# Four or three of eight pairs of row tiles by seven block products, two of the weight sums by accumulating transfers, the second norm's rows on GpSimd's queue, and the hand-over to the MLP in another order

## The chip, the cores and the metric

The kernel runs on one core of a Trainium2 chip. A core has five engines, each with its own in-order queue of instructions: TensorE (PE, matrix products; its weight loads are listed apart as PEld), VectorE (DVE), ScalarE (ACT), GpSimd (POOL) and SyncE (SP, which here only issues transfers). Sixteen DMA engines move data between the device memory and the on-chip memory SBUF; products are summed in a second on-chip memory, PSUM. The metric is the device time of one execution in microseconds. The kernel before takes 1110.16 us, the median of three runs between 1109.35 and 1111.19.

## The reference

One encoder layer over 256 tokens of width 2048 in float32. The part that the change touches is the end of the cross attention, the norm behind it and the MLP:

```
xa = memory_cross_attention(x, layer_norm(mem))          # 4 heads, 256 memory tokens
x  = layer_norm(ALPHA * x + xa)                          # the second norm, "ln2"
ff = jnp.square(jax.nn.relu(x @ w_mlp_in)) @ w_mlp_out   # 2048 -> 8192 -> 2048
x  = layer_norm(ALPHA * x + ff)
```

## The kernel before

**Three products for one.** A float32 matrix product is made of three products of operands split in a rounded high part and a rest: high by high, high by low, low by high. `split` (L78) makes the parts of a tile: ScalarE copies the high part (L80), VectorE subtracts it from the source for the low part (L81). `mm3` (L145) issues the three matmuls. So every weight passes through ScalarE and VectorE once before TensorE uses it. The split weights lie in four buffers each of `w_hi` and `w_lo`, 1024 columns wide.

**The MLP.** The 8192 hidden columns go in four chunks of 2048. For each chunk, four hidden groups (`hidden_group`, L854) compute 512 hidden columns each, transposed, as `ht`: per step of 128 rows of the input, four matmuls of 512 columns and four of 256 (`cols_wide`, L195 and L200). Then two pair products (`pair_product`, L904) multiply the chunk's `ht` into one half (1024 columns) of the output each; in the last chunk the second half goes another way (`w_ml`). A pair product runs over the chunk's sixteen row tiles in eight pairs, called units here. Within a unit, tokens (two blocks of 128), row tiles (two) and columns (two blocks of 512) form a 2 x 2 by 2 x 2 block product. Plainly that is eight block products of three matmuls each. For the units that `SEVEN` (L810) lists, Strassen's scheme in Winograd's form takes seven block products, with sums of blocks of `ht` (`sums_h`, made once per chunk in `hidden`, L832) and sums of blocks of the weights (made by VectorE in `load_unit`, L886). Before, units 2, 5 and 7 of both halves go by seven.

**The weight sums.** A unit's weights are one transfer of 128 x 2048 float32 (1 MB): the blocks b12, b11, b22, b21, 512 columns each. A seven unit needs b11 + b12 and b22 + b12 (one instruction over 1024 columns), that first sum plus b22 (512), and that plus b21 (512). They go into one of two buffers of 2048 columns in `wx`, and then through `split` like weights. The seven unit splits 1024 + 512 + 1024 + 1024 columns, a plain one twice 1024. Transfers of unit p + 2 are issued when unit p begins; the adds are queued then and taken one at a time behind each split (`part`, L893).

**The hand-over.** Between cross attention and the first hidden group stands the second norm. Its work is written out by hand and kept in this order (`pin`): the last cross products (L698) with their sums and statistics per token block (`add_cross`); mean and reciprocal root per block, the root on GpSimd (`moments_pinned`, L702 to L709); `scale2(b, n)` (L716), which normalises columns 512 n to 512 n + 511 of token block b in place on VectorE; `turn2(b, p)` (L728), two transposes on TensorE of the columns of pair p; `convert(p)`, gain and bias of the two transposed tiles (`gain2`, L733 on ScalarE, L735 on VectorE) and their split into `x2t` (L745, or L80 and L81). Pair p covers columns 256 p to 256 p + 255, so that pairs 4 and 5 need the scaled columns n = 2. `first_pair(p)` runs behind the matmuls of input tiles 2 p and 2 p + 1 of the first hidden group: it transposes pairs 2 and 3 of block 1 (p = 0), then pairs 4 to 7. Ten matmuls on a tile of ones (L768) fill TensorE's wait for the moments of block 1.

**The rest of the order.** What isn't pinned is placed by a scheduler that goes by estimated times. `residual("ln2")` (L544) applies gain and bias of the second norm to `res` in 512 columns at a time, with both rows loaded into scratch tiles by SyncE (L551); its pieces are taken one by one behind the splits of the first chunk.

## Time and profile before

| what | value |
|---|---|
| median of three runs | 1110.16 us |
| the profiled execution, its own time | 1108.42 us |
| its span, first to last instruction | 1106.6 us |
| TensorE busy, matmuls | 1091.8 us, 99%, 5951 |
| VectorE busy | 861.1 us, 78% |
| ScalarE busy | 587.3 us, 53% |
| GpSimd busy | 35.6 us, 3% |
| DMA, mean | 195 GB/s, queue share 54.5% of 16 engines |

The profile is one execution. Times within it are microseconds from its first instruction. Matmuls follow each other in a pipeline, so that the busy time of one (389 ns for 512 columns in the groups) is longer than the distance between two; the distance is read from the chain of waits. The chain is the work that ended last, followed back from the last instruction through whatever released it.

### The profile page before, as it was taken

To read this page: it belongs to the slowest core of one execution; us is meant where nothing else is said; L and a number is where in the kernel's file an instruction comes from. 1 tells how busy PE (TensorE), PEld (TensorE's weight loads), DVE (VectorE), ACT (ScalarE), POOL (GpSimd) and SP (SyncE) were. 2 spreads that over 40 slices of the span, in tenths; PEclk is the share of its full clock that TensorE was granted. 3 is DMA by queue.
4 is the path that set the end of the run, shared out by engine and by line. 5 is a ranking of instruction groups with operands and counts; after the bars stand their busy time and mean duration, and the time that the engine had idled before them with its cause. 6 is when DMAs were issued, how large, how long until landed. Compare 5 with 4: busy or idle time off the path is not lost.

```text
span 1106.6 us, 15304 instructions
## 1 busy us (share of the span) xinstructions
PE 1091.8 (99%) x5951; PEld 944.8 (85%) x5951; DVE 861.1 (78%) x1261; ACT 587.3 (53%) x860; POOL 35.6 (3%) x45
## 2 busy tenths in 40 slices
PE   9999999999999999999999999999999999999996
PEld 6988899988999878888888888888888888888885
DVE  6878677688879678888977678978668887678796
ACT  6455566545576435455655445555445555545550
POOL 1402000000100000000000000000000000000000
PEclk9999999999999999999999999999999999999998
DMA  9664453467567318744556555455554556555372
GB/s 333 234 227 142 156 193 127 174 220 247 180 205 272 145 44 299 266 166 181 192 223 221 184 185 209 181 200 192 198 183 175 204 200 223 186 191 190 115 255 87
DMA packets 37944, 215.86 MB, mean 195 GB/s; under 512 B 4336, under 2 KB 5232, under 8 KB 14192
## 3 DMA queue, kind: packets, MB, share of 16 engines
q1 hardware_dynamic: 37872, 214.89, 54.5%
q8 instruction: 46, 0.75, 0.3%
q14 instruction: 26, 0.21, 0.1%
HBM read 212.78 MB, written 2.10 MB: 194 GB/s over the span
## 4 chain that ended last, share of the span: by engine, by line
PE 98%; DVE 1%; DMA 0%; ACT 0%; issue 0%; POOL 0%; DVEq 0%; SPq 0%
PE acc L146 15%; PE acc L147 15%; PE acc L148 15%; PE acc L195 11%; PE att L195 11%; PE att L200 5%; PE acc L200 5%; PE att L147 3%; PE att L148 3%; PE att L146 3%; PE acc L188 2%; PE acc L186 2%; PE acc L187 2%; PE att L350 1%; PE acc L698 1%; PE att L528 1%
## 5 line engine op out<-in xcount | busy, mean ns | idle before, releaser
L81 DVE TENSOR_TENSOR w_lo<-raw,w_hi 128x1024 fp32r<-128x1024 f32 (+2 forms) x318 | 365.9, 1163 | 123.7 <-ACT w_hi L80 118.8
L80 ACT ACTIVATE w_hi<-raw 128x1024 fp32r<-128x1024 f32 (+2 forms) x318 | 317.9, 1011 | 266.0 <-PE acc L148 101.9
L80 ACT ACTIVATE w_hi<-wx 128x1024 fp32r<-128x1024 f32 x98 | 100.8, 1031 | 119.4 <-PE acc L148 85.5
L81 DVE TENSOR_TENSOR w_lo<-wx,w_hi 128x1024 fp32r<-128x1024 f32 x98 | 114.8, 1182 | 53.9 <-ACT w_hi L80 53.8
L195 PE MATMUL att<-x2t,w_hi 128*128 128x512 f32 x512 | 139.6, 394 | 0.0
L147 PE MATMUL acc<-w_lo,ht 128*128 128x512 f32 x354 | 137.8, 389 | 0.0
L148 PE MATMUL acc<-w_hi,ht 128*128 128x512 f32 x354 | 137.7, 389 | 0.0
L195 PE MATMUL acc<-x2t,w_hi 128*128 128x512 f32 x480 | 132.4, 394 | 0.0
L146 PE MATMUL acc<-w_hi,ht 128*128 128x512 f32 x354 | 111.5, 389 | 0.0
L195 PEld LDWEIGHTS att<-x2t,w_hi 128*128 128x128 f32 x512 | 88.0, 189 | 12.3
L195 PEld LDWEIGHTS acc<-x2t,w_hi 128*128 128x128 f32 x480 | 82.5, 189 | 11.5
L200 PEld LDWEIGHTS att<-x2t,w_lo 128*128 128x128 f32 x512 | 77.6, 189 | 10.3
L200 PEld LDWEIGHTS acc<-x2t,w_lo 128*128 128x128 f32 x480 | 73.3, 189 | 9.5
L200 PE MATMUL att<-x2t,w_lo 128*128 128x256 f32 x512 | 80.3, 281 | 0.0
L147 PEld LDWEIGHTS acc<-w_lo,ht 128*128 128x128 f32 x354 | 66.4, 188 | 14.0 <-DVE w_lo L81 0.2
L148 PEld LDWEIGHTS acc<-w_hi,ht 128*128 128x128 f32 x354 | 66.5, 188 | 13.8
L146 PEld LDWEIGHTS acc<-w_hi,ht 128*128 128x128 f32 x354 | 66.4, 188 | 13.8
L200 PE MATMUL acc<-x2t,w_lo 128*128 128x256 f32 x480 | 77.0, 281 | 0.0
L148 PE MATMUL acc<-w_hi,xt 128*128 128x512 f32 (+2 forms) x192 | 69.9, 365 | 0.0
L147 PE MATMUL acc<-w_lo,xt 128*128 128x512 f32 (+2 forms) x192 | 69.7, 364 | 0.0
L146 PE MATMUL acc<-w_hi,xt 128*128 128x512 f32 (+2 forms) x192 | 66.4, 366 | 0.8 <-ACT w_hi L80 0.8
L148 PE MATMUL acc<-w_hi,ot 128*128 128x512 f32 (+1 forms) x136 | 51.9, 382 | 0.0
(259 smaller groups left out, 1873.1 us busy)
## 6 DMA issues: line engine op xcount, KB each, us to landing
raw<-in_w_mi SPq DMA_DIRECT2D x64, 1024.0 KB, 4.9
wx<-in_w_mo SPq DMA_DIRECT2D x28, 1024.0 KB, 4.9
raw<-in_w_mo SPq DMA_DIRECT2D x28, 1024.0 KB, 4.8
raw<-in_w_out SPq DMA_DIRECT2D x16, 1024.0 KB, 4.9
raw<-in_w_ml SPq DMA_DIRECT2D x8, 1024.0 KB, 4.9
raw<-in_w_b SPq DMA_DIRECT2D x5, 1024.0 KB, 4.9
raw<-in_w_qa SPq DMA_DIRECT2D x16, 256.0 KB, 5.4
raw<-in_w_qa SPq DMA_DIRECT2D x4, 1024.0 KB, 4.8
```

The lines of the kernel that those rows point to most:

```text
L80: pin(nc.scalar.activation(hi, src, AF.Copy), pinned)
L81: return pin(nc.vector.tensor_tensor(out=lo, in0=src, in1=f(hi), op=ALU.subtract), pinned)
L146: nc.tensor.matmul(ps, ah, bh, start=start, stop=False)
L147: nc.tensor.matmul(ps, ah, bl, start=False, stop=False)
L148: nc.tensor.matmul(ps, al, bh, start=False, stop=stop)
L186: nc.tensor.matmul(ps, hi, xt[:, k, 0:S], start=k == 0, stop=False)
L187: nc.tensor.matmul(ps, hi, xt[:, k, S:2 * S], start=False, stop=False)
L188: nc.tensor.matmul(ps, lo, xt[:, k, 0:S], start=False, stop=k == nk - 1)
L195: pin(nc.tensor.matmul(ps, hi[:, i * P:(i + 1) * P], xt[:, k, :], start=k == 0, stop=k == nk - 1), pinned)
L200: pin(nc.tensor.matmul(ps[:, 0:S], lo[:, i * P:(i + 1) * P], xt[:, k, 0:S], start=False, stop=False), pinned)
L350: nc.tensor.transpose(pp[:, st * S + b * P:st * S + b * P + P], ev[:, b, st * P:(st + 1) * P], ident)
L528: nc.tensor.transpose(ps[:, o:o + P], x(b, k // 4)[:, (k % 4 + j) * P:(k % 4 + j + 1) * P], ident)
```

## The change

`SEVEN` becomes units 1, 3, 5, 7 of the first half and 3, 5, 7 of the second: 4 x 4 + 3 x 3 = 25 seven units where there were 7 x 3 = 21. `sums_h` holds four pairs.

The sums b11 + b12 and b22 + b12 are made by transfers: SyncE loads b12 twice, side by side, into one of three buffers of 1024 columns, and GpSimd issues a transfer with `accum_op=ALU.add` that adds b11 and b22 from the device memory onto it. `load_halves` does both; it is called before hidden groups 1, 2 and 3 of the first chunk and at the end of each seven unit, for the third seven unit ahead. A seven unit's own transfer leaves b12 out (768 KB). The other two sums stay on VectorE and go into one buffer, `t24`; they are queued during the unit before.

GpSimd's queue, and no longer SyncE's, issues the gain and bias rows of the second norm. In the hand-over `scale2(0, 2)` stands behind the moments of block 1, `scale2(0, 3)` in `first_pair(1)`, `scale2(1, 1)` ahead of `convert(0)` and `scale2(1, 2)` behind `convert(3)`; `convert(0)` uses another division of work between VectorE and ScalarE, `convert(1)` the general one; nine matmuls on ones stand where ten stood.

```diff
@@ residual @@
-                nc.sync.dma_start(rows[w], t[f"{name}_{w}"][n * 512:(n + 1) * 512].partition_broadcast(P))
+                (nc.gpsimd if name == "ln2" else nc.sync).dma_start(rows[w], t[f"{name}_{w}"][n * 512:(n + 1) * 512].partition_broadcast(P))
@@ moments_pinned(st, beside=None) @@
+        if beside is not None:
+            beside()
@@ convert @@
-        if p < 2:
-            for j in range(2):
-                k, o = 2 * p + j, slice(j * S, (j + 1) * S)
-                gain2(x2t[:, k, 0:S], ps[:, o], k, True)
-                gain2(y[:, o], ps[:, o], k, False)
-                pin(nc.vector.tensor_tensor(out=x2t[:, k, S:2 * S], in0=y[:, o],
-                                            in1=f(x2t[:, k, 0:S]), op=ALU.subtract), True)
+        if p == 0:
+
+            gain2(y[:, 0:S], ps[:, 0:S], 0, False)
+            gain2(y[:, S:2 * S], ps[:, S:2 * S], 1, True)
+            pin(nc.vector.tensor_copy(x2t[:, 0, 0:S], y[:, 0:S]), True)
+            pin(nc.scalar.activation(x2t[:, 1, 0:S], y[:, S:2 * S], AF.Copy), True)
+            for j in range(2):
+                pin(nc.vector.tensor_tensor(out=x2t[:, j, S:2 * S], in0=y[:, j * S:(j + 1) * S],
+                                            in1=f(x2t[:, j, 0:S]), op=ALU.subtract), True)
@@ the hand-over @@
-    scale2(0, 2)
-    scale2(0, 3)
     last = cross_mm(1, 3, 256, 256)
...
-    mom[1] = moments_pinned(sts[1])
+    mom[1] = moments_pinned(sts[1], lambda: scale2(0, 2))
...
     turn2(1, 1)
+    scale2(1, 1)
     convert(0)
-    scale2(1, 1)
     convert(1)
@@ first_pair @@
             convert(2)
+            convert(3)
             scale2(1, 2)
-            convert(3)
...
             if p == 1:
+                scale2(0, 3)
                 scale2(1, 3)
@@ the MLP @@
-    SEVEN = ((2, 5, 7), (2, 5, 7))
+    SEVEN = ((1, 3, 5, 7), (3, 5, 7))
...
+    sevens = deque(u for u in units if u[2] in SEVEN[u[1]])
+    t24 = sums_w[0][:, 0:1024]
+    spare = deque([sums_w[0][:, 1024:2048], sums_w[1][:, 0:1024], sums_w[1][:, 1024:2048]])
+
+    def load_halves():
+
+        if not sevens:
+            return
+        c, q, p = sevens.popleft()
+        s, src = spare[0], t["w_mo"][(c * 2 + q) * (CH // 2) + p]
+        spare.rotate(-1)
+        nc.sync.dma_start(s.rearrange("p (i c) -> p i c", i=2),
+                          src[:, 0:512][:, None, :].broadcast_to([P, 2, 512]))
+        nc.gpsimd.dma_start(s, src[:, 512:1536], accum_op=ALU.add)
+        halves.append(s)
@@ load_unit @@
+        o = 512 if seven else 0
+        nc.sync.dma_start(raw[:, o:], t["w_mo"][(c * 2 + q) * (CH // 2) + p][:, o:])
+        s, todo = None, []
         if seven:
-            add(s[:, 0:1024].rearrange("p (i c) -> p i c", i=2), raw[:, 512:1536].rearrange("p (i c) -> p i c", i=2),
-                b12[:, None, :].broadcast_to([P, 2, 512]))
-            add(s[:, 1024:1536], s[:, 0:512], b22)
-            add(s[:, 1536:2048], s[:, 1024:1536], b21)
+            s = halves.popleft(), t24
+            b22, b21 = raw[:, 1024:1536], raw[:, 1536:2048]
+            for o, a, b in ((t24[:, 0:512], s[0][:, 0:512], b22), (t24[:, 512:1024], t24[:, 0:512], b21)):
+                todo.append(lambda o=o, a=a, b=b: nc.vector.tensor_tensor(out=o, in0=a, in1=b, op=ALU.add))
```

What the scheduler makes of it, at three places. The first is VectorE at the start of the hand-over, from the statistics of columns 1536 to 1791 of token block 1 on; `res_1487` is token block 0, `res_1488` block 1. Before:

```order
L500 BN_STATS bn<-res_1488 128x6
L716 TENSOR_SCALAR res_1487<-res_1487,mv,rs_r 128x512 x2
L682 SCALAR_TENSOR_TENSOR res_1488<-res_1488,acc 128x256
L500 BN_STATS bn<-res_1488 128x6
L704 BN_AGGR mv<-bn 128x2
L706 TENSOR_SCALAR rs_v<-mv 128x1
L716 TENSOR_SCALAR res_1488<-res_1488,mv,rs_r 128x512
L735 TENSOR_SCALAR tmp<-att,gbt 128x256
L745 TENSOR_TENSOR x2t<-tmp,x2t 128x256
```

In the changed kernel, from the same statistics on:

```order
L500 BN_STATS bn<-res_1488 128x6
L682 SCALAR_TENSOR_TENSOR res_1488<-res_1488,acc 128x256
L500 BN_STATS bn<-res_1488 128x6
L704 BN_AGGR mv<-bn 128x2
L706 TENSOR_SCALAR rs_v<-mv 128x1
L718 TENSOR_SCALAR res_1487<-res_1487,mv,rs_r 128x512
L718 TENSOR_SCALAR res_1488<-res_1488,mv,rs_r 128x512 x2
L737 TENSOR_SCALAR tmp<-att,gbt 128x256
L746 CAST x2t<-tmp 128x256
L749 TENSOR_TENSOR x2t<-tmp,x2t 128x256 x2
```

The two scalings of block 0 that stood ahead of the last sum (L682) are gone from there: one stands behind the moments, the other much later. Two scalings of block 1 now stand together ahead of the first gain.

The second place is VectorE a little later, around the scaling of columns 1024 to 1535 of block 1 that pair 4 needs; each gain (`tmp<-att,gbt`) with the subtraction behind it is one `convert`. Before, from `convert(2)` on:

```order
L735 TENSOR_SCALAR tmp<-att,gbt 128x256
L81 TENSOR_TENSOR x2t<-tmp,x2t 128x2x256
L716 TENSOR_SCALAR res_1488<-res_1488,mv,rs_r 128x512
L735 TENSOR_SCALAR tmp<-att,gbt 128x256
L81 TENSOR_TENSOR x2t<-tmp,x2t 128x2x256
L81 TENSOR_TENSOR w_lo<-raw,w_hi 128x1024
```

In the changed kernel, from `convert(2)` on:

```order
L737 TENSOR_SCALAR tmp<-att,gbt 128x256
L81 TENSOR_TENSOR x2t<-tmp,x2t 128x2x256
L737 TENSOR_SCALAR tmp<-att,gbt 128x256
L81 TENSOR_TENSOR x2t<-tmp,x2t 128x2x256
L718 TENSOR_SCALAR res_1488<-res_1488,mv,rs_r 128x512
L81 TENSOR_TENSOR w_lo<-raw,w_hi 128x1024
```

The scaling moved from between `convert(2)` and `convert(3)` to behind both. On TensorE nothing moved there: the transposes of pair 4 stand behind the matmuls of input tiles 2 and 3 in both kernels.

The third place is the transfers of the first chunk. SyncE before, from the last of seven `w_mi` loads on:

```order
L134 DMA raw<-in_w_mi 128x2048 x7
L551 DMA tmp<-in_ln_g 128x512
L551 DMA tmp<-in_ln_b 128x512
L551 DMA tmp<-in_ln_g 128x512
L878 DMA wx<-in_w_mo 128x2048 x2
L134 DMA raw<-in_w_mi 128x2048
```

SyncE in the changed kernel, from the same loads on:

```order
L134 DMA raw<-in_w_mi 128x2048 x7
L884 DMA wx<-in_w_mo 128x2x512 x3
L897 DMA wx<-in_w_mo 128x2048
L897 DMA wx<-in_w_mo 128x1536
L134 DMA raw<-in_w_mi 128x2048 x7
L897 DMA raw<-in_w_mo 128x2048
```

GpSimd in the changed kernel, from the roots of the second norm on (before, nothing but two later roots followed them):

```order
L711 TENSOR_TENSOR rs_r<-rs_v,mhalf 128x1 x2
L551 DMA tmp<-in_ln_g 128x512
L551 DMA tmp<-in_ln_b 128x512
L551 DMA tmp<-in_ln_g 128x512
L886 DMA wx<-in_w_mo 128x1024 x2
L551 DMA tmp<-in_ln_b 128x512
L886 DMA wx<-in_w_mo 128x1024
```

The rows of the norm left SyncE's queue, where the doubled loads of b12 now stand ahead of the weights of units 0 and 1 and of the next `w_mi` loads; on GpSimd the rows share the queue with the accumulating transfers.

## Rows read from the trace of the kernel before

**Rows 1.** The page of the kernel before: the span, the row of TensorE (busy us, share of the span, instructions), the granted clock in tenths by fortieths of the span, the chain that ended last, by engine, and the loads of `w_mi` (count, size of one, us from issue to landing).

```profile
span 1106.6 us, 15304 instructions
...
PE 1091.8 (99%) x5951; PEld 944.8 (85%) x5951; DVE 861.1 (78%) x1261; ACT 587.3 (53%) x860; POOL 35.6 (3%) x45
...
PEclk9999999999999999999999999999999999999998
...
PE 98%; DVE 1%; DMA 0%; ACT 0%; issue 0%; POOL 0%; DVEq 0%; SPq 0%
...
raw<-in_w_mi SPq DMA_DIRECT2D x64, 1024.0 KB, 4.9
```

**Rows 2.** Busy time by stretch, for the first chunk's hidden groups after the hand-over, the two pair products of the first chunk, and the hidden groups of the second chunk. Columns: the stretch, its length, busy us and instruction count of PE, of the weight loads (PEld), DVE, ACT and POOL, then the granted clock, the share of the 16 DMA engines and GB/s.

```profile
410.00:492.00 82.00, 82.00 (x473) 71.79 (x472) 66.57 (x105) 43.92 (x65) 0.00 (x0) 1.00 0.68 241
492.00:534.00 42.00, 42.00 (x187) 34.78 (x186) 36.36 (x50) 24.92 (x33) 0.00 (x0) 1.00 0.48 182
534.00:576.00 42.00, 42.00 (x189) 34.83 (x188) 36.23 (x41) 23.52 (x28) 0.00 (x0) 1.00 0.56 201
575.00:664.00 89.00, 89.00 (x510) 77.89 (x509) 63.45 (x93) 43.67 (x61) 0.00 (x0) 1.00 0.56 195
```

**Rows 3.** The chain of waits in order of time around the two pinned cross-attention products: start, length, what (x36 are 36 matmuls of 512 columns, one behind the other).

```profile
382.96 8.17 PE acc L698 x36
```

**Rows 4.** The timeline of the hand-over from the second norm to the first hidden group: start us, busy us, engine, line, operation, out<-in, count, and in brackets the idle time before it and what ended it.

```profile
393.71 0.28 PE L698 MATMUL acc<-w_hi,attC 128*128 128x256 f32 x1
...
394.19 0.98 DVE L716 TENSOR_SCALAR res<-res,mv,rs_r 128x512 f32<-128x512 f32 x2
...
395.09 0.41 DVE L682 SCALAR_TENSOR_TENSOR res<-res,acc 128x256 f32<-128x256 f32 x1
...
396.56 0.54 POOL L709 TENSOR_TENSOR rs_r<-rs_v,mhalf 128x1 f32<-128x1 f32 x1 [5.34 <-DVE rs_v L706]
...
397.14 0.55 DVE L716 TENSOR_SCALAR res<-res,mv,rs_r 128x512 f32<-128x512 f32 x1 [0.66 <-POOL rs_r L709]
...
397.74 0.66 PE L728 MATMUL att<-ident,res 128*128 128x128 f32 x4 [0.71 <-DVE res L716]
398.21 0.56 ACT L733 ACTIVATE x2t<-att,gbt 128x256 fp32r<-128x256 f32 x1 [14.15 <-PE att L728]
398.81 0.54 DVE L735 TENSOR_SCALAR tmp<-att,gbt 128x256 f32<-128x256 f32 x1 [1.13 <-ACT x2t L733]
399.39 0.42 DVE L745 TENSOR_TENSOR x2t<-tmp,x2t 128x256 fp32r<-128x256 f32 x1
...
399.96 1.17 PE L195 MATMUL acc<-x2t,wide 128*128 128x512 f32 x4 [1.57 <-ACT x2t L733]
...
402.84 0.60 PE L728 MATMUL att<-ident,res 128*128 128x128 f32 x4
...
403.26 0.56 ACT L733 ACTIVATE tmp<-att,gbt 128x256 f32<-128x256 f32 x1 [0.76 <-PE att L728]
403.86 0.54 DVE L735 TENSOR_SCALAR tmp<-att,gbt 128x256 f32<-128x256 f32 x1 [0.32 <-ACT tmp L733]
...
405.10 0.69 DVE L81 TENSOR_TENSOR x2t<-tmp,x2t 128x512 fp32r<-128x512 f32 x1 [0.70 <-ACT x2t L80]
...
405.71 0.54 DVE L716 TENSOR_SCALAR res<-res,mv,rs_r 128x512 f32<-128x512 f32 x1
...
406.08 0.66 PE L728 MATMUL att<-ident,res 128*128 128x128 f32 x4
406.16 0.54 DVE L735 TENSOR_SCALAR tmp<-att,gbt 128x256 f32<-128x256 f32 x1
...
406.50 1.18 PE L195 MATMUL acc<-x2t,wide 128*128 128x512 f32 x4
...
407.40 0.69 DVE L81 TENSOR_TENSOR x2t<-tmp,x2t 128x512 fp32r<-128x512 f32 x1 [0.70 <-ACT x2t L80]
```

**Rows 5.** Groups of instructions by line and shape on VectorE: count, then busy us and mean ns of one, then the idle time before them.

```profile
L81 DVE TENSOR_TENSOR w_lo<-raw,w_hi 128x1024 fp32r<-128x1024 f32 x280 | 339.7, 1223 | 119.5 <-ACT w_hi L80 115.0 <-PE acc L200 2.7
...
L81 DVE TENSOR_TENSOR w_lo<-raw,w_hi 128x512 fp32r<-128x512 f32 x30 | 20.6, 699 | 3.1 <-ACT w_hi L80 2.7
...
L886 DVE TENSOR_TENSOR wx<-wx,raw 128x512 f32<-128x512 f32 x28 | 19.1, 682 | 0.0
...
L886 DVE TENSOR_TENSOR wx<-raw 128x1024 f32<-128x1024 f32 x14 | 17.1, 1222 | 1.8 <-DMA raw<-in_w_mo 1.5
...
L344 DVE TENSOR_SCALAR tmp<-tmp,rz 128x256 f32<-128x256 f32 x40 | 12.5, 358 | 0.6
```

**Rows 6.** Busy time by stretch again (columns as in rows 2), for 15 us of the first chunk's second hidden group.

```profile
430.00:435.00 5.00, 5.00 (x30) 4.34 (x29) 5.00 (x12) 4.11 (x9) 0.00 (x0) 1.00 0.94 264
435.00:440.00 5.00, 5.00 (x31) 4.38 (x30) 5.00 (x10) 2.12 (x2) 0.00 (x0) 1.00 1.01 429
440.00:445.00 5.00, 5.00 (x30) 4.34 (x29) 5.00 (x6) 2.03 (x2) 0.00 (x0) 1.00 0.98 342
```

**Rows 7.** The timeline of the transfers that SyncE issues (columns as in rows 4), in the first chunk.

```profile
434.09 0.33 SPq L134 DMA_DIRECT2D raw<-in_w_mi  x1
```

**Rows 8.** The timeline of ScalarE in the first chunk (columns as in rows 4).

```profile
448.24 1.06 ACT L80 ACTIVATE w_hi<-raw 128x1024 fp32r<-128x1024 f32 x1
...
452.50 1.06 ACT L80 ACTIVATE w_hi<-raw 128x1024 fp32r<-128x1024 f32 x1 [1.10 <-PE acc L195]
```

More of the change, by code (lines that the diff above doesn't have):

```diff
@@ L700, in cross_mm, with moments_pinned @@
         return ps
-    def moments_pinned(st):
+    def moments_pinned(st, beside=None):
         mv = small.tile([P, 2], F32, tag="mv", name="mv")
@@ L766, in encoder_kernel @@
     pst[3] = att_tile()
-    for _ in range(10):
+    for _ in range(9):
         pin(nc.tensor.matmul(pst[3], ones, ones[:, None, :].broadcast_to([P, 4, P]),
@@ L813, in encoder_kernel @@
     ht = big3("ht")
-    sums_h = late.tile([P, 3072], F32R, name="sums_h").rearrange("p (u l c) -> p u l c", l=2, c=512)
+    sums_h = late.tile([P, 4096], F32R, name="sums_h").rearrange("p (u l c) -> p u l c", l=2, c=512)
     wx = big.tile([P, 8192], F32, tag="big", name="wx")
@@ L877, in load_unit @@
         raw = raw2[p % 4] if p % 4 < 2 else raw_tile()
[L878 to L879 removed]
+        o = 512 if seven else 0
+        nc.sync.dma_start(raw[:, o:], t["w_mo"][(c * 2 + q) * (CH // 2) + p][:, o:])
+        s, todo = None, []
         if seven:
[L881 to L891 removed]
+            s = halves.popleft(), t24
+            b22, b21 = raw[:, 1024:1536], raw[:, 1536:2048]
+            for o, a, b in ((t24[:, 0:512], s[0][:, 0:512], b22), (t24[:, 512:1024], t24[:, 0:512], b21)):
+                todo.append(lambda o=o, a=a, b=b: nc.vector.tensor_tensor(out=o, in0=a, in1=b, op=ALU.add))
+        loaded.append((raw, s, todo))
     def part(src):
@@ L910, in pair_product @@
             load_unit(c)
-            raw, s = loaded.popleft()
+            raw, s, _ = loaded.popleft()
+            if loaded:
+                sums.extend(loaded[0][2])
             k = 2 * p
@@ L972, in encoder_kernel @@
             first = c == 0 and g == 0
+            if c == 0 and 0 < g:
+                load_halves()
             if g == CH // G - 1:
```

15 lines of the change are left out of this document (4 added, 11 removed).

## The prediction

> **What bounds the kernel now.** I read the page first. TensorE is busy for 99% of the span, its clock is granted at nine tenths or more nearly to the end, and the chain that ended last is TensorE for 98% [rows 1]. Busy matmuls overlap, so that alone doesn't prove a bound; the stretches do. From 410 us on TensorE is busy in every microsecond of the hidden groups and of both pair products, with 36.4 us of VectorE and 24.9 us of ScalarE in 42 us [rows 2]. So in the MLP only matmuls taken away, or new waits, change the time. The distance between two matmuls of 512 columns is 8.17 / 36 = 0.227 us [rows 3]. The one place nearby where TensorE stands still is the hand-over: 0.71 us for a scaled tile and 1.57 us for the first converted one [rows 4].
>
> **Matmuls removed.** Four more seven units, each 21 matmuls for 24: 4 x 3 x 0.227 = 2.72 us, on the path, since nothing else is awaited there. The order has 13 matmuls fewer; the thirteenth is one on ones, and it filled a wait, so it counts nothing: eight or nine, TensorE still gets to the transposes before the scaled tile is there.
>
> **The hand-over, up to the first matmul.** The last cross product ends at 393.71 + 0.28 = 393.99. Before, VectorE then did two scalings of block 0 from 394.19 on and began the last sum at 395.09 [rows 4]. Now this sum begins at 394.19, and all that follows comes 0.90 us sooner: the root at 395.66, the scaling of block 1 at 396.24 for 397.14. The scaling of block 0 that now stands behind the moments lies beside the 0.54 us of the root. The transposed tile was read 398.21 - 397.14 = 1.07 us after that scaling began, so now at 397.31; the second scaling of block 1, put in between, ends by then (0.98 us for two in a row). Then come the gain on VectorE (398.81 to 399.39 in steps: 0.58), the copy of the high part, which the trace doesn't show in this form, and the subtraction (0.42); the first matmul began 0.15 us after its end. For the copy the rows next to it are a one-operand instruction on 256 columns, 0.36 [rows 5], and the subtraction's 0.42; half of a 0.55 us scaling, 0.27, is the other end. I take 0.36: 397.31 + 0.58 + 0.36 + 0.42 + 0.15 = 398.82, that is 1.14 us sooner than 399.96.
>
> **The hand-over, behind it.** Here a gain turns into a new wait. Pair 4's transposes stand behind input tiles 2 and 3, and need columns 1024 to 1535 of block 1 scaled. Before, that scaling ended at 405.71 + 0.54 = 406.25, just as TensorE came to the transposes (406.08), and the next matmuls began 0.25 later, at 406.50 [rows 4]. Now the scaling stands behind `convert(3)`. Gains of ScalarE and VectorE that read one PSUM tile follow each other (403.26, then 403.86, released by ScalarE), so `convert(2)` and `convert(3)` are a chain: from ScalarE's gain at 403.26 to the second subtraction at 407.40. Without the scaling between them (VectorE's gain at 405.71 instead of 406.16, 0.45 us) this subtraction begins at 406.95, and a scaling behind it, 0.61 us later as 405.71 is behind 405.10, ends at 408.10: 4.84 us after ScalarE's gain. In the changed kernel the transposes before this gain begin 2.88 us after the first matmul, as 402.84 after 399.96, and the gain 0.42 later: 398.82 + 3.30 = 402.12. The scaling ends at 406.96, the next matmuls begin at 407.21. TensorE comes to the transposes at 398.82 + 6.12 = 404.94, so it waits about 2 us, and is 407.21 - 406.50 = 0.71 us later than before. Later scalings have more room: those of columns 1536 on end some 4 us after this one and are wanted two groups of matmuls, 6 us, after it. I take +0.71. Bounds: if nothing waits there, the whole 1.14 is kept (-1.14); if the first matmul gains nothing and the wait is the same, +1.85.
>
> **VectorE and ScalarE in the MLP.** Each seven unit loses a 1024-column add (1.22), each added one brings 1536 more columns to split (1.22 + 0.70) and two adds of 0.68 [rows 5]. First-half product: +3.28 - 3 x 1.22 = -0.4 us on 36.4, in 180 x 0.227 = 40.9 us of TensorE; second half -3.7. One more set of sums of `ht` per chunk, five instructions of at most 0.68, falls into hidden groups where VectorE has 89.0 - 63.5 us free [rows 2]. All this is hidden behind TensorE: 0. It can't go below nothing, since TensorE waits for neither engine there. If the cover went, the added 0.70 and 1.22 us would show per unit, 4 x 3.28 = 13 us at most.
>
> **DMA, steady.** A first-half product moved 182 GB/s x 42 us = 7.6 MB at a share of 0.48, the second 8.4 MB at 0.56 [rows 2]: 2.6 to 2.8 us of all sixteen engines per MB. Now it moves 4 x 1.05 + 4 x 0.79 + 4 x 0.52 (b12 written twice) = 9.4 MB, 26.4 us, and four accumulating transfers of 0.52 MB. The trace has none of these. At a plain load's price they take 1.5 us each, and 32 of 40.9 us are used. Cover: splits run ahead of TensorE by four buffers until TensorE frees one [rows 8], three of them still full, 3 x 12 x 0.227 = 8.2 us. So they may take (40.9 + 8.2 - 26.4) / 4 = 5.7 us each, nearly four times a load, before TensorE waits. I take 0.
>
> The Trainium skill, Collectives: The Full Stack, section The bandwidth ceiling, says that an add within a DMA engine needs two reads per chunk and runs at half the rate of a copy. No row here shows it; by it the sum would be the same, since 26.4 + 4 x 2.9 = 38 us still fit.
>
> **DMA, first chunk.** From 430 to 445 us the sixteen engines are busy at 0.94 to 1.01 [rows 6]. There the change adds three doubled loads and three accumulating ones, less the 0.26 MB of b12: 2.9 MB, 8 us, or 12.5 if an accumulation costs double. SyncE's `w_mi` load of 434.09 [rows 7] now queues behind 3.3 MB. It lands in 4.9 us [rows 1], and ScalarE wanted it at 448.24 [rows 8]: 9.2 us of room, and 8.2 more before TensorE notices. On GpSimd, behind an accumulating transfer that waits for its first half stand rows of the norm; VectorE waits for these, and all splits behind it, with the same 8.2 us of cover. 0 again; up to 3 us if the covers fail together.
>
> The Trainium skill, DMA: Bandwidth & Descriptors, section Issuing engines are not separate DMA queues, says that transfers run on the same sixteen engines whoever issues them. The share near 1 in rows 6 is in its sense, though all transfers there are SyncE's; by it the rows' new queue shortens no transfer, by the opposite the stretch would be freer, and the sum is the same by both.
>
> **Sum.** -2.72 + 0.71 = -2.0 us on the profiled execution's 1108.42 us (span 1106.6 and 1.8 around it): 1106.4. That execution is 1.7 us under the median, so for the median 1110.16 - 2.0 = 1108.2 us, -0.18%. What a measurement of this kernel can tell from no change is about 0.2%, 2.2 us: the forecast lies just inside.
>
> **Rivals.**
> A, the forecast: 1107.4 to 1109.2 by the bounds on the copy and half a microsecond on the wait. For it: every step has its row.
> B, no wait at pair 4, because gains on one tile don't follow each other in the new division or VectorE gets there earlier: -2.72 - 1.14 = -3.9, 1106.3. Against it: the releases in rows 4, and the order of VectorE.
> C, slower: accumulating transfers hold the DMA engines so long that weights and sums come late to VectorE, which stops all splits. It decides from 5.7 us each. At six times a load's 1.5 us, 8.8 us, each first-half product lacks 26.4 + 4 x 8.8 - 49.1 = 12.5 us, four of them 50: about 1158; at 6.3 us each 4 x 4 x 0.6 = 10 us, 1118. For it: nothing of this kind has run in this program. Against it: the free half of the engines.
> D, the change in the main does what it says, but new small waits (first chunk, norm rows, the changed order of unpinned work) give 1 to 3 us back: 1109.2 to 1111.2.
>
> **Chances.** A 0.50, B 0.18, C 0.13, D 0.19. Faster by over 0.2% are B and four tenths of A (beyond -2.2 us): 0.38. Slower by over 0.2% are C and a few outliers of D: 0.16. Within 0.2%: 0.46. The range reaches from a little under B, 1106.0, to the upper end of D and the mildest of C, 1112.0; about 0.1 is left out above and less than 0.1 below.
>
> **What would show it.** The count of matmuls is 5938, and TensorE's chain in a first-half product has 180 of them. The timeline of the hand-over has the first wide matmul near 1.1 us earlier relative to the last cross product, and then a wait of about 2 us of TensorE for a scaled tile ahead of pair 4, which the list of TensorE's waits didn't have. In stretches of pair products TensorE stays fully busy, the DMA share rises to 0.7 to 0.9, and VectorE's 1024-column adds are gone. I am wrong if TensorE waits for weight parts in the MLP, if an accumulating transfer takes over 5 us, or if there is no wait at pair 4.

## The result and the profile after

The changed kernel takes 1111.68 us (median of 16 executions, 1110.72 to 1113.67), the kernel before on the same chip 1110.32 us (1108.25 to 1112.72). The ratio is 1.0017, 95% interval 1.0010 to 1.0024: slower, by about 0.17%. The forecast was 1108.2 us, 2.0 us less than before; measured are 1.4 us more.

The profiled executions are 1111.96 us after and 1108.42 before, further apart (3.5 us) than the medians (1.4): that execution of before is one of its short ones. The stages below come from the profiled executions.

From the page of the changed kernel: span, TensorE's row, GpSimd's queue (packets, MB, share of sixteen engines' span), the chain that ended last, by engine, and the adding transfers (count, size of one, median us from issue to landing).

```profile
span 1109.9 us, 15446 instructions
...
PE 1091.6 (98%) x5938; PEld 939.7 (85%) x5938; DVE 854.4 (77%) x1274; ACT 593.6 (53%) x872; POOL 64.9 (6%) x78
...
q0 software_dynamic: 4240, 15.21, 7.3%
...
PE 88%; DVE 5%; DMA 3%; ACT 2%; issue 1%; SPq 0%; POOL 0%; DVEq 0%; ACTq 0%
...
wx<-in_w_mo POOLq DMA_DIRECT2D x25, 512.0 KB, 8.7
```

The matmuls are the 5938 that were forecast, and VectorE's adds of 1024 columns [rows 5] are gone. What changed is the chain: TensorE alone was 98% of it [rows 1], now 88%, and VectorE and DMA have 8% between them. So TensorE now waits in more places than before.

The starts of TensorE's stages in the timeline say where. Each column is the distance between first matmuls: A from the last cross product to the first wide matmul of pair 4 (the hand-over), B from there to the first pair product (the first chunk's hidden groups), C the two pair products of a chunk (mean of chunks 1 to 3), D the hidden groups of chunks 2 to 4 (mean), E the last chunk's pair product to the first matmul that is `w_ml`'s. The sum is A + B + 3C + 3D + E.

| kernel | A | B | C | D | E | sum | ratio to before, 95% |
|---|---|---|---|---|---|---|---|
| before | 12.79 | 85.50 | 82.96 | 89.74 | 61.10 | 677.5 | |
| changed | 13.62 | 88.14 | 82.82 | 90.18 | 60.39 | 681.2 | 1.0017 (1.0010 to 1.0024) |
| `e1_scale_back` | 11.77 | 86.23 | 82.82 | 90.18 | 60.39 | 677.4 | 0.9984 (0.9975 to 0.9993) |
| `e2_halves_spread` | 13.61 | 87.26 | 82.83 | 90.18 | 60.40 | 680.3 | 1.0009 (1.0000 to 1.0018) |
| `e3_adds_pinned` | 13.61 | 87.98 | 82.29 | 89.74 | 60.39 | 678.1 | 0.9990 (0.9982 to 0.9999) |
| `e4_all_three` | 11.77 | 86.22 | 82.28 | 89.74 | 60.40 | 674.5 | 0.9954 (0.9940 to 0.9968) |
| `e5_before_handover` | 13.62 | 85.55 | 83.23 | 89.74 | 61.53 | 679.6 | 1.0010 (1.0001 to 1.0019) |
| `e6_before_25` | 12.78 | 85.50 | 82.77 | 89.74 | 60.34 | 676.2 | 0.9988 (0.9979 to 0.9997) |
| `e7_rows_on_sync` | 13.62 | 94.57 | 82.81 | 90.20 | 60.39 | 687.6 | 1.0077 (1.0065 to 1.0090) |
| `e8_no_accumulate` | 13.62 | 85.98 | 82.82 | 90.20 | 60.39 | 679.1 | 0.9999 (0.9990 to 1.0008) |
| `e9_back_and_pinned` | 11.78 | 85.55 | 82.28 | 89.74 | 60.39 | 673.8 | 0.9950 (0.9937 to 0.9963) |
| `e11_old_handover` | 14.33 | 85.93 | 82.83 | 90.21 | 60.40 | 679.8 | 0.9993 (0.9984 to 1.0003) |
| `e12_one_load_later` | 13.63 | 85.50 | 82.83 | 90.20 | 60.40 | 678.6 | 0.9994 (0.9985 to 1.0002) |
| `e13_back_pinned_later` | 11.77 | 85.48 | 82.28 | 89.74 | 60.40 | 673.7 | 0.9946 (0.9934 to 0.9958) |

Against before the changed kernel loses 0.83 us in A, 2.64 in B and 1.3 in D (3 x 0.44), and gains 1.1 in C and E together where the twelve removed matmuls should give 2.7. That is 3.7 us; the span grew by 3.2, since the work behind E is 0.7 us shorter, for a reason that wasn't looked for, and the work ahead of A 0.2 longer.

**A, the hand-over.** The timeline of the changed kernel there; its columns are those of [rows 4], whose rows it answers to.

```profile
393.95 0.28 PE L698 MATMUL acc<-w_hi,attC 128*128 128x256 f32 x1
...
396.70 1.00 DVE L718 TENSOR_SCALAR res<-res,mv,rs_r 128x512 f32<-128x512 f32 x2 [0.44 <-POOL rs_r L711]
397.30 0.66 PE L730 MATMUL att<-ident,res 128*128 128x128 f32 x4 [0.25 <-DVE res L718]
...
398.36 0.29 DVE L746 CAST x2t<-tmp 128x256 fp32r<-128x256 f32 x1
...
399.17 1.20 PE L195 MATMUL acc<-x2t,wide 128*128 128x512 f32 x4 [1.21 <-DVE x2t L749]
...
406.78 0.54 DVE L718 TENSOR_SCALAR res<-res,mv,rs_r 128x512 f32<-128x512 f32 x1
...
407.37 0.44 PE L730 MATMUL att<-ident,res 128*128 128x128 f32 x2 [1.69 <-DVE res L718]
407.57 1.18 PE L195 MATMUL acc<-x2t,wide 128*128 128x512 f32 x4
```

The first wide matmul stands 5.22 us behind the last cross product, 6.25 before: 1.03 us sooner. Then TensorE waits 1.69 us for the scaled tile (`res`, L718) ahead of pair 4, where it had no wait, and is 0.83 us late. The gain turned into a larger wait.

**B, the first chunk.** The timeline of SyncE's transfers (it answers to [rows 7]), of ScalarE [rows 8] and of TensorE.

```profile
428.17 2.99 SPq L884 DMA_DIRECT2D wx<-in_w_mo  x3
431.22 2.00 SPq L897 DMA_DIRECT2D wx<-in_w_mo  x2
434.74 29.77 SPq L134 DMA_DIRECT2D raw<-in_w_mi  x5
...
452.96 1.06 ACT L80 ACTIVATE w_hi<-raw 128x1024 fp32r<-128x1024 f32 x1 [9.55 <-DMA raw<-in_w_mi]
...
462.88 0.73 PE L200 MATMUL acc<-x2t,w_lo 128*128 128x256 f32 x4 [1.41 <-DVE w_lo L81]
```

The weight load of 434.74 is behind three doubled loads and the loads of units 0 and 1. ScalarE waits 9.55 us for it, to 452.96. In the kernel before, the same load is that of 434.09 [rows 7]. The two issues, before and after (count, KB, us from issue to landing), and the split that used the load's first half before:

```profile
raw<-in_w_mi SPq DMA_DIRECT2D x1, 1024.0 KB, 8.9
...
raw<-in_w_mi SPq DMA_DIRECT2D x1, 1024.0 KB, 18.1
...
444.04 1.06 ACT L80 ACTIVATE w_hi<-raw 128x1024 fp32r<-128x1024 f32 x1 [1.69 <-PE att L195]
```

The load took 8.9 us already before, when 4.9 was the median over the whole kernel, and landed at 443.0. A load is split in two halves, and the two splits from it are the 145th and 146th of ScalarE's copies of `raw` in both kernels: 452.96 and 454.98 after, 444.04 and 448.24 before. So before it came 1.0 us ahead of its use. The stretches of this time (columns as in [rows 2]; they answer to [rows 6]):

```profile
435.00:440.00 5.00, 5.00 (x32) 4.39 (x31) 3.69 (x8) 1.53 (x2) 2.36 (x3) 1.00 1.03 381
...
445.00:450.00 5.00, 5.00 (x31) 4.44 (x30) 3.28 (x6) 0.00 (x0) 0.57 (x1) 1.00 1.05 310
450.00:455.00 5.00, 4.86 (x27) 3.93 (x25) 0.95 (x1) 2.04 (x6) 0.00 (x0) 1.00 1.03 360
455.00:460.00 5.00, 4.93 (x27) 3.81 (x26) 5.00 (x12) 3.33 (x6) 0.00 (x0) 1.00 0.96 312
460.00:465.00 5.00, 3.59 (x22) 2.88 (x21) 5.00 (x10) 2.97 (x6) 0.77 (x2) 1.00 0.71 256
```

The DMA engines are full to 455. ScalarE does nothing from 445 to 450, and VectorE little from 450 to 455. From 455 to 465 VectorE is busy in all ten microseconds with what has gathered, and only there, at 462.88, does TensorE's largest wait of the chunk come: the loss is paid ten microseconds behind its cause.

**C and D, the pair products and later chunks.** VectorE's and TensorE's timeline at the head of the first chunk's second pair product, and at the head of the second chunk:

```profile
534.46 1.28 DVE L959 SCALAR_TENSOR_TENSOR res<-res,acc 128x512 f32<-128x512 f32 x2
535.66 0.69 DVE L903 TENSOR_TENSOR wx<-wx,raw 128x512 f32<-128x512 f32 x1
536.26 2.35 DVE L81 TENSOR_TENSOR w_lo<-wx,w_hi 128x1024 fp32r<-128x1024 f32 x2
...
537.53 0.50 PE L147 MATMUL acc<-w_lo,ht 128*128 128x512 f32 x1 [0.18 <-DVE w_lo L81]
...
577.66 0.69 DVE L903 TENSOR_TENSOR wx<-wx 128x512 f32<-128x512 f32 x1
578.26 2.35 DVE L81 TENSOR_TENSOR w_lo<-raw,w_hi 128x1024 fp32r<-128x1024 f32 x2
...
579.53 0.39 PE L200 MATMUL acc<-x2t,w_lo 128*128 128x256 f32 x1 [0.18 <-DVE w_lo L81]
```

In the kernel before, at the head of the first chunk's second product:

```profile
531.38 1.28 DVE L943 SCALAR_TENSOR_TENSOR res<-res,acc 128x512 f32<-128x512 f32 x2
532.58 2.35 DVE L81 TENSOR_TENSOR w_lo<-wx,w_hi 128x1024 fp32r<-128x1024 f32 x2
```

L903 is a weight sum that is wanted later. It stands between the sums of the finished products (L959), which have to come first, and the split of the next weights (L81), for which TensorE is waiting; before, nothing stood there. Each such place costs some 0.5 us by the distances between starts in C and D, more than the idle 0.18 of the row, since the busy time of a matmul is longer than its distance to the next. There are six, three at heads of second products and three at heads of chunks.

The theory from these rows: three separate waits, one made by the scaling's place, one by transfers crowded in the first chunk, one by the order of VectorE's adds.

### The profile page after: what moved, and what is told of

Same layout as the page of the kernel before. It is cut to its first block, busy times and chain, and to the rows that moved or that the text cites. A ratio compares the mean times of both kernels' runs of the same rounds, so it can differ in the third digit from the quotient of the medians.

```text
span 1109.9 us, 15446 instructions
## 1 busy us (share of the span) xinstructions
PE 1091.6 (98%) x5938; PEld 939.7 (85%) x5938; DVE 854.4 (77%) x1274; ACT 593.6 (53%) x872; POOL 64.9 (6%) x78
## 3 DMA queue, kind: packets, MB, share of 16 engines
q0 software_dynamic: 4240, 15.21, 7.3%
## 4 chain that ended last, share of the span: by engine, by line
PE 88%; DVE 5%; DMA 3%; ACT 2%; issue 1%; SPq 0%; POOL 0%; DVEq 0%; ACTq 0%
PE acc L147 13%; PE acc L148 13%; PE acc L146 13%; PE att L195 10%; PE acc L195 10%; PE acc L200 5%; PE att L200 5%; PE att L148 3%; PE att L147 3%; PE att L146 3%; DVE w_lo L81 2%; PE acc L188 2%; PE acc L186 2%; PE acc L187 2%; DMA raw<-in_w_mi 2%; ACT w_hi L80 1%
## 5 line engine op out<-in xcount | busy, mean ns | idle before, releaser
L81 DVE TENSOR_TENSOR w_lo<-raw,w_hi 128x1024 fp32r<-128x1024 f32 (+2 forms) x318 | 365.6, 1161 | 129.5 <-ACT w_hi L80 127.1
L81 DVE TENSOR_TENSOR w_lo<-wx,w_hi 128x1024 fp32r<-128x1024 f32 x106 | 122.9, 1167 | 63.2 <-ACT w_hi L80 62.4
L80 ACT ACTIVATE w_hi<-wx 128x1024 fp32r<-128x1024 f32 x106 | 106.0, 1015 | 109.9 <-PE acc L148 76.1
L147 PE MATMUL acc<-w_lo,ht 128*128 128x512 f32 x330 | 128.8, 390 | 0.5 <-DVE w_lo L81 0.5
L148 PE MATMUL acc<-w_hi,ht 128*128 128x512 f32 x330 | 128.5, 389 | 0.0
L146 PE MATMUL acc<-w_hi,ht 128*128 128x512 f32 x330 | 101.9, 389 | 0.0
L147 PEld LDWEIGHTS acc<-w_lo,ht 128*128 128x128 f32 x330 | 61.9, 188 | 14.7 <-DVE w_lo L81 2.0
L146 PEld LDWEIGHTS acc<-w_hi,ht 128*128 128x128 f32 x330 | 61.9, 188 | 13.3 <-DVE res L962 0.4
L148 PEld LDWEIGHTS acc<-w_hi,ht 128*128 128x128 f32 x330 | 61.9, 188 | 12.8
L886 POOL DMA_DIRECT2D wx<-in_w_mo x25 | 21.7, 869 | 544.5 <-DVE wx L903 269.6
```

The source lines that it names most:

```text
L80: pin(nc.scalar.activation(hi, src, AF.Copy), pinned)
L81: return pin(nc.vector.tensor_tensor(out=lo, in0=src, in1=f(hi), op=ALU.subtract), pinned)
L146: nc.tensor.matmul(ps, ah, bh, start=start, stop=False)
L147: nc.tensor.matmul(ps, ah, bl, start=False, stop=False)
L148: nc.tensor.matmul(ps, al, bh, start=False, stop=stop)
L886: nc.gpsimd.dma_start(s, src[:, 512:1536], accum_op=ALU.add)
```

## The experiments

### The scaling back between two conversions (`e1_scale_back`)

```diff
             convert(2)
+            scale2(1, 2)
             convert(3)
-            scale2(1, 2)
```

> The changed kernel with the scaling of columns 1024 to 1535 of block 1 back between convert(2) and convert(3). The theory (three separate waits of TensorE: at pair 4, for the first chunk's late weights, and behind the weight sums that the scheduler puts at the heads of products and chunks) expects the wait of 1.7 us ahead of pair 4's transposes to go, the first hidden group's tile 8 to begin about 1.9 us sooner after the last cross product than in the changed kernel, and the whole to take 1.5 to 2 us less than the changed kernel, ratio to the kernel before 0.9998 to 1.0004. The rival (the first chunk's late weights set the pace, and an earlier hand-over only runs into them sooner) expects the wait to go but the time to stay within 0.5 us of the changed kernel's, ratio 1.0015, with 1.5 us more of waits for weights between 440 and 470 us.

A falls to 11.77, so the wait at pair 4 is gone and the 1.03 us of the hand-over are kept. But B fell too, by 1.9 us, which neither the theory nor the rival had, and the ratio, 0.9984, lies below both ranges. The edit also changed what the scheduler made of SyncE's queue: one weight load (433.01 us) now stands between the loads of units 0 and 1, which had stood together. So the first two waits aren't separate.

### The doubled loads spread (`e2_halves_spread`)

The first three doubled loads and the loads of units 0 and 1 are kept in program order among pinned instructions, which sets some of them behind weight loads.

```diff
-        nc.sync.dma_start(s.rearrange("p (i c) -> p i c", i=2),
-                          src[:, 0:512][:, None, :].broadcast_to([P, 2, 512]))
+        pin(nc.sync.dma_start(s.rearrange("p (i c) -> p i c", i=2),
+                              src[:, 0:512][:, None, :].broadcast_to([P, 2, 512])), first)
...
-        nc.sync.dma_start(raw[:, o:], t["w_mo"][(c * 2 + q) * (CH // 2) + p][:, o:])
+        pin(nc.sync.dma_start(raw[:, o:], t["w_mo"][(c * 2 + q) * (CH // 2) + p][:, o:]),
+            (c, q) == (0, 0) and p < 2)
...
```

> The changed kernel with the first chunk's three doubled loads, and the loads of units 0 and 1, kept on SyncE's queue behind the weight loads that stand before them in the program. The theory expects ScalarE's wait of 9.6 us for a weight load near 450 us to shrink to under 3 us, TensorE to stay busy from 440 to 495 us, the first chunk's hidden groups to take 2.6 us less, and a ratio to the kernel before of 0.9990 to 0.9998. The rival (the norm rows on GpSimd's queue behind accumulating transfers, not the amount of transfers, hold VectorE and so the splits) expects VectorE still to wait there and less than 0.7 us gained, ratio 1.0010 to 1.0017.

Only 0.9 us came back in B, and the ratio lies between the two ranges. The timeline of GpSimd's transfers and of VectorE in this kernel says why:

```profile
436.38 1.92 POOL L886 DMA_DIRECT2D wx<-in_w_mo  x2 [2.28 <-DMA wx<-in_w_mo]
438.02 0.84 POOL L551 DMA_DIRECT2D tmp<-in_ln_b  x1
454.82 0.85 POOL L886 DMA_DIRECT2D wx<-in_w_mo  x1 [15.96 <-DMA wx<-in_w_mo]
...
453.47 1.29 DVE L555 TENSOR_TENSOR res<-res,tmp 128x512 f32<-128x512 f32 x2 [8.51 <-DMA tmp<-in_ln_b]
```

The weights now come in time (ScalarE's longest wait for them is 2.9 us), but VectorE waits 8.51 us, to 453.47, for a norm row that GpSimd issued at 438.02, behind two adding transfers: 15 us for a row. The third adding transfer holds up GpSimd's queue for another 15.96 us, until its doubled load, now later, has landed. One late transfer was traded for another.

### The sums pinned behind their splits (`e3_adds_pinned`)

```diff
-todo.append(lambda o=o, a=a, b=b: nc.vector.tensor_tensor(out=o, in0=a, in1=b, op=ALU.add))
+todo.append(lambda o=o, a=a, b=b: pin(nc.vector.tensor_tensor(out=o, in0=a, in1=b, op=ALU.add), True))
```

> The changed kernel with VectorE's two weight sums of a seven unit kept behind the split they follow in the program. The theory expects the six waits of about 0.5 us of TensorE at the start of second products and of chunks (two each in chunks 1 to 3 of four) to go: pair products of 82.3 us per chunk instead of 82.8, hidden groups of 89.7 instead of 90.2, 2.5 to 3 us in all, ratio to the kernel before 0.9988 to 0.9998. The rival (those waits come from the drained sums or from late weights, the adds only stand near them) expects the waits to stay at the same places and a ratio of 1.0010 to 1.0020.

VectorE at the head of the second product in this kernel:

```profile
534.40 1.28 DVE L959 SCALAR_TENSOR_TENSOR res<-res,acc 128x512 f32<-128x512 f32 x2
535.60 2.35 DVE L81 TENSOR_TENSOR w_lo<-wx,w_hi 128x1024 fp32r<-128x1024 f32 x2
```

The add has gone from there and all six waits with it: C is 82.29, D 89.74 as before. C and E together are now 2.7 us under before (3 x 0.67 + 0.71), the whole of the removed matmuls.

### The three together (`e4_all_three`)

The edits of the three kernels above in one.

> The three edits of the other runs together. If the three waits are separate, their gains add up: 1.9 + 2.6 + 2.8 = 7.3 us less than the changed kernel, about 1104.5 us, ratio to the kernel before 0.9942 to 0.9962, and TensorE's list of waits from 400 us on is as empty as that of the kernel before. If one wait hides another, less: ratio 0.997 to 0.999.

The waits of A, C and D are gone. B stays 0.7 us above before.

### The hand-over alone (`e5_before_handover`)

The kernel before with the changed `moments_pinned`, `convert` and order of scalings: the front's diff of these places and no other.

> The kernel before with the new hand-over alone (lines of moments_pinned, convert and the order of scalings), three seven units and all sums on VectorE as before. Theory (the hand-over costs by its own wait at pair 4): the first matmul of the MLP stands 1.0 us sooner, a wait of 1.7 to 2 us ahead of pair 4, all later work 0.7 to 0.9 us later, pair products at 82.96 us and hidden groups at 89.74 us as before: ratio 1.0004 to 1.0012. Rival (the moved scaling also makes the scheduler issue the weight loads of the first chunk later, whatever is added to the DMA queues): 1 to 2 us more are lost in the first chunk, ratio 1.0015 to 1.0028.

A is that of the changed kernel and B nearly that of before: without the added transfers the first chunk loses nothing. The rival falls. What the expectation didn't have are 0.8 us in the third chunk's products and 0.4 in E. In the first of these places a unit's transfer landed 6.0 us after its issue, at 848.2, where it took 4.7 before, and VectorE waited 1.72 us for it with the sums and splits behind it, in the same order as before. Whether the new hand-over has to do with it isn't shown.

### The seven units alone (`e6_before_25`)

```diff
-    SEVEN = ((2, 5, 7), (2, 5, 7))
+    SEVEN = ((1, 3, 5, 7), (3, 5, 7))
```

and `sums_h` of 4096 columns, in the kernel before.

> The kernel before with four, then three seven units alone: the 12 wide matmuls are gone, and all sums are VectorE's, as before. Theory A (the adds stand in front of urgent splits because unit 1, the second of a product, now has sums, whoever makes the others): the six places of about 0.5 us are there, or longer since VectorE has 3.3 us more to do in a first-half product, and eat what the matmuls give: ratio 0.9990 to 1.0015. Theory B (those waits come only with the sums that DMAs make): pair products of a chunk take 82.3 us instead of 82.96 and hidden groups stay at 89.74: -2.7 us, ratio 0.9970 to 0.9982.

The measure is between the two. VectorE at the head of the second product:

```profile
531.52 0.68 DVE L886 TENSOR_TENSOR wx<-wx,raw 128x512 f32<-128x512 f32 x1
532.12 0.68 DVE L943 SCALAR_TENSOR_TENSOR res<-res,acc 128x512 f32<-128x512 f32 x1
532.72 2.35 DVE L81 TENSOR_TENSOR w_lo<-wx,w_hi 128x1024 fp32r<-128x1024 f32 x2
```

A sum (L886 here) stands ahead of the split here too, and C is 82.77, 0.48 more than with pinned sums: the three waits at second products come with the seven units themselves, as theory A has it. D is 89.74, without loss: the three at heads of chunks don't, as theory B has it. VectorE's larger load (it makes all sums here) shows no other cost in the stages.

### The norm rows on SyncE's queue (`e7_rows_on_sync`)

```diff
-                (nc.gpsimd if name == "ln2" else nc.sync).dma_start(rows[w], ...
+                nc.sync.dma_start(rows[w], ...
```

> The changed kernel with the norm rows back on SyncE's queue. Theory (the first chunk's loss is late weights, because more bytes stand ahead of them; the rows on GpSimd's queue are waited for too, but beside it): no gain, 87.5 to 89 us from pair 4's matmuls to the pair products against 88.14, ratio to the kernel before 1.0010 to 1.0025. Rival (rows behind accumulating transfers hold VectorE and by that the splits): 1 to 2.6 us come back, 85.5 to 87, ratio 0.9993 to 1.0008.

Both were wrong: B grew by 6.4 us. SyncE's transfers in this kernel, and two stretches of it:

```profile
429.66 1.02 SPq L897 DMA_DIRECT2D wx<-in_w_mo  x2
430.72 0.86 SPq L551 DMA_DIRECT2D tmp<-in_ln_g  x1
431.62 1.38 SPq L551 DMA_DIRECT2D tmp<-in_ln_b  x1
433.10 0.80 SPq L551 DMA_DIRECT2D tmp<-in_ln_g  x1
435.43 0.33 SPq L134 DMA_DIRECT2D raw<-in_w_mi  x1
```

```profile
455.00:460.00 5.00, 1.20 (x4) 0.67 (x4) 5.00 (x13) 3.09 (x5) 0.00 (x0) 0.89 0.98 408
460.00:465.00 5.00, 3.80 (x13) 3.42 (x14) 5.00 (x10) 3.15 (x4) 0.00 (x0) 0.50 0.55 187
```

Three rows now stand ahead of the weight load as well. TensorE is busy for 1.20 of 5 us from 455 on, and the granted clock is 0.50 in the next stretch, so that some of the 6.4 us is clock; how much isn't shown. The move of the rows to GpSimd's queue, which the prediction gave no gain, is what keeps the changed kernel from this.

### The adding transfers without the add (`e8_no_accumulate`)

```diff
-        nc.gpsimd.dma_start(s, src[:, 512:1536], accum_op=ALU.add)
+        nc.gpsimd.dma_start(s, src[:, 512:1536])
```

> The changed kernel with each accumulating transfer replaced by a plain load of the same bytes on the same queue; it leaves the block product b12 out of the two weight sums. Theory (bytes crowd the first chunk, not the accumulation): the transfers still land in over 8 us between 430 and 465 us, and of the 2.6 us lost there at most 1 comes back: ratio 1.0008 to 1.0018; the six waits behind adds stay. Rival (the accumulation itself is what is slow): the transfers land in under 5 us, the DMA share falls below 0.9 in that stretch and 1.5 to 2.6 us come back: ratio 0.9993 to 1.0004.

The rival holds in the time, though not in its signs. SyncE's order is unchanged (weight load at 434.66 us, behind the same transfers) and so are the bytes, yet 2.16 of the 2.64 us of B come back. From the page of this kernel, GpSimd's queue and its weight transfers:

```profile
q0 software_dynamic: 4240, 15.21, 4.3%
...
wx<-in_w_mo POOLq DMA_DIRECT2D x25, 512.0 KB, 6.2
```

The same 15.21 MB take 4.3% of 1107.7 us, 47.6 us of all sixteen engines, and 7.3% of 1109.9, 81.0 us, with the add: 33.4 / 25 = 1.3 us more for each transfer. The eight rows of the norm on this queue are 2.1 of the 15.21 MB; taken at one price per byte in the run without the add, and at the same time in both runs, they leave an estimate of 3.0 us for a transfer with the add and 1.6 without, a factor of 1.8. The rival's landing under 5 us and a DMA share under 0.9 between 435 and 455 did not come (11.5 us in that stretch, 1.01 to 1.03).

### With the old hand-over (`e11_old_handover`)

The changed kernel with the old `moments_pinned`, `convert` and order of scalings.

> The changed kernel with the old hand-over (moments, conversions and the order of scalings as before); seven units, adding transfers and rows on GpSimd's queue stay. SyncE then issues one weight load between the loads of units 0 and 1, as with the scaling back. Theory (the new hand-over's order put that weight load behind unit 1's, and with the accumulations this made the weights late): pair 4's matmuls at 406.5 us as before, 86.0 to 86.5 us from there to the pair products instead of 88.14, the six waits behind adds stay: ratio 0.9994 to 1.0009. Rival (the accumulating transfers are late whatever the order): 87.5 us or more, ratio 1.0009 to 1.0022.

B is 85.93: with the weight load between units 0 and 1 the added transfers cost 0.4 us and not 2.64. The ratio is just below the theory's range. A, 14.33, is no measure of the order: the granted clock fell there, which the last section shows.

### One load later (`e12_one_load_later`)

Unit 1's load of 768 KB is issued behind four weight loads; hand-over, accumulations and sums stay.

```diff
-                load_unit(c)
+                if c > 0:
+                    load_unit(c)
...
+            def weights(k):
+                w = s_in.next()
+                if s_in.n == 17:
+                    load_unit(0)
+                return w
...
```

(that load and the ninth weight load of the stream are pinned, so that they stay in this order)

> The changed kernel, hand-over kept, with unit 1's load of 768 KB moved behind four weight loads on SyncE's queue. Theory (what is late are the weight loads behind it): 86.0 to 87.0 us from pair 4's matmuls to the pair products instead of 88.14, pair 4 at 407.5 as in the changed kernel, ratio 1.0000 to 1.0012. Rival (0.79 MB more or less ahead of the weights does not matter while three accumulations run; the scaling's place helped in another way): 87.5 us or more, ratio 1.0012 to 1.0024.

SyncE's transfers and ScalarE in this kernel:

```profile
434.39 20.25 SPq L134 DMA_DIRECT2D raw<-in_w_mi  x4
454.69 0.42 SPq L898 DMA_DIRECT2D wx<-in_w_mo  x1
...
448.84 1.06 ACT L80 ACTIVATE w_hi<-raw 128x1024 fp32r<-128x1024 f32 x1 [5.78 <-DMA raw<-in_w_mi]
```

ScalarE still waits, 5.78 us, but TensorE doesn't: B is 85.50, that of before. One transfer's place on SyncE's queue is the whole 2.64 us, with all accumulations in place; the theory had expected half a microsecond or more to stay, and the ratio, 0.9994, is just below its range.

### What beats both (`e9_back_and_pinned`, `e13_back_pinned_later`)

The scaling back and the sums pinned, without spreading; and the same with unit 1's load later.

> The changed kernel with the scaling back between the two conversions and the two sums pinned behind the splits that they follow, without spreading the doubled loads. Theory (the three waits are separate, and the scaling's place alone also brings the weight load of the first chunk forward): the edits add up, 405.4 us for pair 4's matmuls, 86.2 us from there to the pair products, 82.28 us of pair products in a chunk, hidden groups 89.74 us: ratio 0.9946 to 0.9964, as with the spreading. Rival (the spreading is what made the sum of the three work): the first chunk takes 87.3 us or more, ratio 0.9964 to 0.9975.

> All of it together: the scaling back, the sums pinned, unit 1's load behind four weight loads. Theory: as the changed kernel with scaling back and sums pinned, with the 0.7 us that the first chunk still takes over the kernel before gone in part: 85.5 to 86.0 us from pair 4's matmuls to the pair products, ratio 0.9942 to 0.9958. Rival (another transfer is late then, a norm row or the third accumulation): 86.2 us or more, ratio 0.9954 to 0.9968.

1104.45 and 1103.78 us beside 1110.09 of before. B is 85.55 already in the first, lower than the 86.2 expected and 0.7 below `e1_scale_back`: there two sums of 0.68 us stand among VectorE's splits behind the late load (456.05 and 458.66 us), here none does. The load's move adds 0.07 us, nothing that these runs tell apart (0.9950 and 0.9946), and the spreading of `e4_all_three` had cost 0.7 us.

## Why the prediction was wrong

The sum was -2.72 + 0.71, with 0 for VectorE and ScalarE in the MLP and 0 for the DMA of the first chunk. Its two priced terms came; the two terms put at 0 cost 2.9 and 2.64 us and turned the sign.

- **Matmuls removed**: right. 2.72 us were forecast, 2.7 appear when nothing else is in the way (`e3_adds_pinned`).
- **The hand-over, up to the first matmul**: right, 1.03 us sooner for 1.14. The copy took 0.29 us, within its bounds of 0.27 and 0.36.
- **The hand-over, behind it**: right, +0.83 for +0.71, with a wait of TensorE of 1.69 us for "about 2". That the place was a choice shows in `e1_scale_back`: the old place gives -1.02.
- **VectorE and ScalarE in the MLP** failed. It counted busy time per product (36.0 us of VectorE in 40.9 of a first-half product) and concluded 0. What cost time was position: one add of 0.69 us ahead of a split that TensorE already waits for, six times, 2.9 us in all (2.7 - 1.1 in C and E, 1.3 in D). At the head of a product no cover is left to hide such an add: without it the waits are gone.
- **DMA, first chunk** failed. It set 8 to 12.5 us of added transfers against 9.2 and 8.2 us of cover and took 0, with "up to 3 us if the covers fail together". 2.64 came. The size of the added transfers was right: the load took 9.2 us longer from issue to landing than before (18.1 for 8.9), within the 8 to 12.5. The first cover was misread, twice. It took the median of all such loads, 4.9 us, for a load that needed 8.9 in this stretch; and it took the split of 448.24 for the first use of the load, which is the one of 444.04. The room was 1.0 us and not 9.2. The second cover isn't free in full either, since VectorE's work gathers in it and has to be done afterwards. Counted from the 444.04 of before, moved by as much as pair 4's matmuls moved, the split came 7.8 us late here for 2.64 us in B, 5.7 late in `e8_no_accumulate` for 0.5, and 4.1 late in `e12_one_load_later` for nothing. By engine time the added transfers are near the expensive end of the range, 8 + 3 x 1.3 = 11.9 us, since the add costs a transfer 1.8 times a load's time. The Trainium skill, Collectives: The Full Stack, section The bandwidth ceiling, puts the adding step of a collective at half a copy's rate, because the add needs two reads. The trace's factor is near that.
- **DMA, steady**: right in its result; with the sums pinned, the products' C is shorter by the matmuls that were removed and has no loss from transfers. Their DMA share was 0.77 and 0.85, as forecast (0.7 to 0.9). But its test was wrong: it held "over 5 us" of an adding transfer to be fatal, and they landed in 8.7 us at the median without harm. The limit of 5.7 us was one of engine time, which is 3.0 by the estimate above; from issue to landing a transfer also waits for others.
- **Rival D** named what happened, small new waits, but gave them 1 to 3 us; the waits of B, C and D took 5.5 (2.64 + 2.9).

The medians are nearer to the forecast than the stages: +1.4 us where the profiled span has +3.2. No term of the prediction has this difference; the last section has a possible reason.

That the accumulations' price and the order on SyncE's queue are both conditions of B is shown by `e8_no_accumulate` and `e12_one_load_later`: taking away either removes most or all of the loss. Why the scheduler put unit 1's load ahead of the weight load with the new place of the scaling wasn't tried.

## What to carry to other kernels

Cover counted in busy time says nothing about the head of a stage: there, look at which instruction stands directly ahead of the one that is waited for, and pin what can wait. Read the landing of a transfer from its own row in its own stretch, not from the median of its kind, and count which instruction uses it first. Where a stretch already has its DMA engines full, the order on the issuing queue can decide: with the same bytes, one load moved was worth 2.6 us. And a change that is slower as a whole may hold its gain in full: here one line moved and one line pinned turned 0.17% slower into 0.5% faster, of which the stages of the table show 3.7 us.
